# Two batches of triangular inverses moved from VectorE to GpSimd, and their closing transposes to a later place

## The chip, the cores and the metric

The kernel runs on one core of a Trainium2 chip. The metric is the device time of one execution in microseconds; less is better. Engines are named as in the profile: PE is TensorE, DVE is VectorE, ACT is ScalarE, POOL is GpSimd, SP is SyncE.

## What is computed

The kernel runs two blocks of a transformer one after the other, all in fp32, with 512 tokens and a width of 1024. The change lies in the mixer of an even layer of the second block. That mixer has two halves that read the same projections: a gated delta rule that runs over the tokens forward and backward, over a context of 256 tokens and the 512 latent tokens, and MLA, a softmax attention of 8 heads. The delta rule is computed in chunks of 64 tokens, and each chunk needs the inverse of a unit triangular matrix:

```python
m = jnp.where(strict, jnp.einsum('bhncd,bhnsd->bhncs', kb, kc) * decay, 0.0)
eye = jnp.eye(cl, dtype=f32)
tmat = lax.linalg.triangular_solve(m + eye, jnp.broadcast_to(eye, m.shape), left_side=True,
                                   lower=True, unit_diagonal=True)
u = jnp.einsum('bhncs,bhnsv->bhncv', tmat, vb)
w = jnp.einsum('bhncs,bhnsk->bhnck', tmat, kb * jnp.exp(gc)[..., None])
...
def step(s, inp):
    u_i, w_i, qk_i, qd_i, kd_i, gl_i = inp
    v_new = u_i - jnp.einsum('bhck,bhkv->bhcv', w_i, s)
    o_i = jnp.einsum('bhck,bhkv->bhcv', qd_i, s) + jnp.einsum('bhcs,bhsv->bhcv', qk_i, v_new)
    s = s * gl_i[..., None, None] + jnp.einsum('bhck,bhcv->bhkv', kd_i, v_new)
    return s, o_i
```

## The kernel before

The even layer's mixer starts with `even_in` (L1136), which runs the projections and convolutions and ends with the projections of L416. Beside its last units run the jobs of `gdn_chunks` (L1430). `decays(b)` (L1448) builds the matrices of one block of 128 tokens, and ScalarE copies their 32 x 32 diagonal parts into a batch tile (`triW`, L1489). There are three batches: "ctx", 0 (four latent blocks forward) and 1 (four backward). `inversion` transposes a batch on VectorE into the tile A (`triangles`, L1500) and inverts it: `invert` clears X and writes ones on its diagonal (L1505, L1506) and then, for j from 0 to 30, with n = j + 1 and m = 31 - j, multiplies a column of A with a row of X into the one buffer `tm` (L1510) and subtracts that from X (L1511), n times m elements on each of 128 partitions. A transpose (L1513) writes the result back into the batch's tile:

```python
t = gp.tile([128, 256], F32, name="tm", bufs=1)[:, :n * m].rearrange("p (y x) -> p y x", y=m)
V.tensor_tensor(t, X[:, j:j + 1, :n].to_broadcast([128, m, n]), A[:, n:, j:j + 1].to_broadcast([128, m, n]), OP.mult)
V.tensor_tensor(X[:, n:, :n], X[:, n:, :n], t, OP.subtract)
```

Batches 0 and 1 are the last job (L1522). Their tiles A and X are borrowed from the tiles eo0, eo1, eo2 (and a part of `triW`) that later hold the mixer's outputs.

`gdn_scan` (L1524) walks over the blocks, forward and backward side by side, in six walks; the walks 0 and 1 take the two context blocks, the walks 2 to 5 the latent blocks, so batches 0 and 1 are needed from walk 2 on. It has four tiles DT, two for each direction, which are cleared once (L1527). `solve(i)` copies the diagonal parts of the inverses into DT (L1546 on ScalarE, eight copies for a pair of blocks), completes them with two rounds of small products (`Dn`, L1556, `ng`, L1559 and L1563), and multiplies (`sa`, L1575). `step` (L1600) is one chunk of one direction, and its last instruction updates the state St (L1633).

Beside the walks runs `mla` (L1380), a generator that is advanced by one or two units after a walk. It goes over four pairs of heads p, and GpSimd issues its DMAs: the values `vp` (L1384, two buffers), the keys and queries `kq` of the two heads (L1388, 576 KB each, two buffers in all), and the stores of the results `boD` (L1419). TensorE computes the scores S (L1402) from kq. The context part of each result is cast into eo1 and eo3 (`hl`, L398 and L399).

The order of each engine's instructions is set by a scheduler that takes the program's instructions by readiness and priority; on the chip each engine then runs its queue in that order, each instruction waiting for what it needs. `tc.issue_after(x)` has the scheduler place what follows behind x.

Of the kernel before, what the change touches and what calls it, by code (L numbers as in the profile page):

```python
# [12 lines left out]
OP = mybir.AluOpType  # L13
# [225 lines left out]
def build(tc, A, out, cst_at, vec_at, chk_at, tap=None, upto=99, mark=lambda n: None):  # L239
    nc = tc.nc  # L240
    V, S, T, G = nc.vector, nc.scalar, nc.tensor, nc.gpsimd
# [53 lines left out]
    def bank(tag, cols, name):  # L295
        p, rings = state["pm"]
        return p.tile([128, cols], F32, name=name, tag=tag, bufs=rings[tag], padded_shape=[128, max(cols, 512)])
# [315 lines left out]
    x = xp.tile([128, KD, SEQ], F32, name="x", tag="x")  # L613
# [805 lines left out]
                    G.dma_start(boD[p, :, qb0:qb0 + 256], bt)  # L1419
                yield  # L1420

    batches, batch, inverse, NOc = {}, {}, {}, []

    def off_diagonal(d, a):

# [4 lines left out]
    def gdn_chunks(gp, slots):  # L1430
# [70 lines left out]

        def invert(key, A, X, Y):

            parts = batches[key][1]
            V.memset(X, 0.0)  # L1505
            V.memset(X.rearrange("p y x -> p (y x)")[:, ::33], 1.0)  # L1506
            for j in range(31):
                n, m = j + 1, 31 - j
                t = gp.tile([128, 256], F32, name="tm", bufs=1)[:, :n * m].rearrange("p (y x) -> p y x", y=m)
                V.tensor_tensor(t, X[:, j:j + 1, :n].to_broadcast([128, m, n]), A[:, n:, j:j + 1].to_broadcast([128, m, n]), OP.mult)  # L1510
                V.tensor_tensor(X[:, n:, :n], X[:, n:, :n], t, OP.subtract)  # L1511
            for d, r in parts:
                V.transpose(Y[r], X[r] if d == 0 else X[r].rearrange("p s c -> p c s"))  # L1513
            inverse[key] = Y

        def inversion(key, A, X):
            triangles(key, A)
            invert(key, A, X, batches[key][0])
# [4 lines left out]

    def gdn_scan(oT, gA, gp, beside, then):  # L1524
        DTs = [[gp.tile([128, 8, 128], F32, name=f"DT{d}{i}") for i in range(2)] for d in range(2)]
        for t in DTs[0] + DTs[1]:
            G.memset(t, 0.0)  # L1527
        prep = {}

        def solve(i):  # L1530
# [69 lines left out]
        def step(d, b, a, St):  # L1600

            u, wT, kd, eb, qd, qk = prep[d, b]
            rows = halves[a]

            pb = bank("step", 1024, "st").rearrange("p (b c) -> p b c", b=2)
            pw, po, pu = pb[:, :, :256], pb[:, a, 256:], pb[:, 1 - a, 256:]
            for p in range(4):
                for r in halves:  # L1610
                    T.matmul(po[r, 64 * p:64 * p + 64], St[r, p], qd[r, p, rows], start=p == 0, stop=False)
            for p in range(4):
                for half, r in enumerate(halves):
                    T.matmul(pw[rows, half, 64 * p:64 * p + 64], wT[r, p, rows], St[r, p], start=half != a, stop=half != a,
                             skip_group_check=half == a)
            vn = gp.tile([128, 8, 64], F32, name="vn", bufs=3)
            by = [v.rearrange("p (i b) t -> p i b t", b=2) for v in (vn[rows], u[rows])]
            V.tensor_tensor(by[0], by[1], pw[rows].rearrange("p b (i t) -> p i b t", i=4), OP.subtract)
            for h in range(8):
                T.matmul(pu[halves[h % 2], 64 * (h // 2):64 * (h // 2) + 64], kd[rows, h], vn[rows, h], start=True, stop=True)  # L1620
            for h in range(8):
                T.matmul(po[halves[h % 2], 64 * (h // 2):64 * (h // 2) + 64], vn[rows, h], qk[rows, 64 * h:64 * h + 64],
                         start=False, stop=h > 5)
            ot = oT[:, :, 128 * b + 64 * a:128 * b + 64 * a + 64]
            o3 = po.rearrange("p (i t) -> p i t", i=4)
            if (b, a) in seen:
                V.tensor_tensor(ot, o3, ot, OP.add)
            else:
                S.copy(ot, o3)
                seen.add((b, a))  # L1630
            last = 64 * a + (63 if d == 0 else 0)
            V.tensor_tensor(St, St, eb[:, :, last:last + 1].to_broadcast([128, 4, 64]), OP.mult)
            V.tensor_tensor(St, pu.rearrange("p (i t) -> p i t", i=4), St, OP.add)  # L1633

        St = []
        for d in range(2):
# [3 lines left out]
        order = [[4, 5, 0, 1, 2, 3], [5, 4, 3, 2, 1, 0]]  # L1640

        def walk(i):
            solve(i)
            for a in range(2):
                for d in range(2):
                    step(d, order[d][i], a if d == 0 else 1 - a, St[d])

        next(beside)
        for i in range(6):
            walk(i)  # L1650
            if i == 3:
                then()
            for _ in range(UNITS[i]):
                next(beside, None)
# [163 lines left out]
    def gated(sl, to, tile, ring, p):  # L1818
# [5 lines left out]
        for i, rb in zip(pairs, rsqrt_bcs(sqs, 2, 64, ring, p)):  # L1824
# [5 lines left out]

    gp = pool("gdn_b", gst, side="right")
    gdn_scan(oT, gA, gp, mla(pool("mla", mst, side="right"), [v[1] for v in os_[SEQ]]),
             lambda: gated(CT, [v[0] for v in os_[SEQ]], lambda n: gp.tile([128, 512], F32, name=n, tag=n, bufs=2), "turn", gp))
    mst.close()
# [52 lines left out]
    def begin(st):  # L1887
# [17 lines left out]
    order = [((4, 5, 6, 7, 8, 9), [CT]), ((0, 1, 2, 3), [PA]), ((1, 2, 3, 0), [PB]), ((10, 11, 16, 17), [LAT, CT]),  # L1905
             ((4, 5, 6, 7, 8, 9, 12, 13, 14, 15), [LAT])]
# [269 lines left out]
```

## Time and profile before

| | |
|---|---|
| median of 3 runs | 3221.37 us (3218.88 to 3226.10) |
| the profiled execution, its own time | 3223.53 us |
| its span | 3221.7 us |
| busy: TensorE, VectorE, ScalarE, GpSimd | 3067.8, 2041.2, 1448.2, 17.4 us |
| share of TensorE, of GpSimd in the chain that ended last | 62%, 0% |

The span is the time from the first to the last recorded instruction, and the profiled execution took 1.8 us more than its span. A row of a timeline gives start, duration, engine, line and operation, the tile written and the tiles read, and in brackets how long the engine stood idle before and what ended that. A row of a table by stretches gives, for one stretch of time, what the columns of its heading say. Each product of two fp32 operands has two records on TensorE.

### The profile page before, as it was taken

The numbers are of one execution on the slowest core, as the hardware profiler recorded it, in microseconds if no ns is written. First come the engines' busy times: TensorE is split into PE (matmuls) and PEld (weight loads), VectorE is DVE, ScalarE is ACT, GpSimd is POOL, SyncE is SP. The second block draws the span as 40 slices with busy tenths as digits, with TensorE's granted clock in tenths as the row PEclk, the third lists the DMA queues.
The fourth block names the chain that finished last, engine by engine and source line by source line (L and its number), as shares of the span: only waits on it lengthen the run. The fifth ranks groups of instructions, "written<-read, shape, count | busy, mean of one in ns | idle before, by whom it ended". The sixth has DMA issues, their size and how long they took to land.

```text
span 3221.7 us, 51374 instructions
## 1 busy us (share of the span) xinstructions
PE 3067.8 (95%) x20678; PEld 2605.9 (81%) x20678; DVE 2041.2 (63%) x4021; ACT 1448.2 (45%) x2533; POOL 17.4 (1%) x47
## 2 busy tenths in 40 slices
PE   6999999998999999998899999999997989999998
PEld 5788888975888889876667898888887867898887
DVE  7976555788787777668966674442338347572335
ACT  4965333446553335556554562212124446562223
POOL 0000000000000000000100000000000000000000
PEclk9999999997999999998999999999998999999999
DMA  7556554320266554442322433441223221242232
GB/s 233 190 155 218 194 189 163 125 66 7 74 195 200 188 198 166 131 143 96 107 67 92 142 105 118 165 136 58 67 69 125 79 91 47 76 152 95 95 100 101
DMA packets 137615, 404.11 MB, mean 125 GB/s; under 512 B 13856, under 2 KB 37152, under 8 KB 136736
## 3 DMA queue, kind: packets, MB, share of 16 engines
q1 hardware_dynamic: 135344, 389.81, 36.6%
q0 software_dynamic: 2032, 11.01, 1.1%
q8 instruction: 162, 2.65, 0.3%
q14 instruction: 77, 0.63, 0.1%
HBM read 376.12 MB, written 24.64 MB: 124 GB/s over the span
## 4 chain that ended last, share of the span: by engine, by line
PE 62%; issue 8%; DVE 5%; ACT 4%; DMA 0%; POOL 0%; DVEq 0%; ACTq 0%; POOLq 0%
PE mm L416 49%; PE po L1359 2%; PE rb L547 2%; PE ptr L1348 1%; PE S L830 1%; PE S L1402 1%; PE ss L527 1%; ACT DT L1546 1%; ACT wH L398 1%; PE po L969 1%; PE sa L1575 1%; PE ptr L975 1%; DVE acc L519 1%; DVE wL L399 1%; DVE ct L1683 0%
## 5 line engine op out<-in xcount | busy, mean ns | idle before, releaser
L398 ACT CAST wH<-raw 128x1024 fp32r<-128x1024 f32 (+4 forms) x446 | 451.8, 1015 | 1144.7 <-PE mm L416 786.0
L399 DVE TENSOR_TENSOR wL<-raw,wH 128x1024 fp32r<-128x1024 f32 (+4 forms) x446 | 525.1, 1180 | 377.4 <-ACT wH L398 370.5
L416 PE MATMUL mm<-mH,wH 128*128 128x256 f32 (+1 forms) x1280 | 406.8, 340 | 8.2 <-DVE f L1764 5.8
L416 PE MATMUL mm<-mH,wL 128*128 128x256 f32 (+1 forms) x1280 | 404.1, 339 | 1.9 <-DVE wL L399 1.9
L416 PE MATMUL mm<-mL,wH 128*128 128x256 f32 (+1 forms) x1280 | 404.2, 338 | 0.0
L416 PEld LDWEIGHTS mm<-mH,wH 128*128 128x128 f32 x1280 | 230.7, 190 | 39.5 <-ACT wH L398 6.0
L589 DVE SCALAR_TENSOR_TENSOR raw<-raw,cond_c 128x1024 f32<-128x1024 f32 x128 | 156.6, 1225 | 157.1 <-DMA raw<-in_ada 156.4
L416 PEld LDWEIGHTS mm<-mH,wL 128*128 128x128 f32 x1280 | 229.7, 189 | 30.9 <-DVE wL L399 2.3
L416 PEld LDWEIGHTS mm<-mL,wH 128*128 128x128 f32 x1280 | 230.2, 189 | 28.6
L416 PE MATMUL mm<-f2u0L,wH 128*128 128x512 f32 (+1 forms) x752 | 190.3, 327 | 0.0
L416 PE MATMUL mm<-f2u0H,wH 128*128 128x512 f32 (+1 forms) x752 | 190.0, 326 | 0.0
L416 PE MATMUL mm<-f2u0H,wL 128*128 128x512 f32 (+1 forms) x752 | 189.6, 326 | 0.0
L416 PE MATMUL mm<-f2u1H,wL 128*128 128x512 f32 (+1 forms) x432 | 151.4, 352 | 1.2 <-DVE wL L399 1.1
L416 PE MATMUL mm<-f2u1H,wH 128*128 128x512 f32 (+1 forms) x432 | 150.9, 352 | 0.6 <-ACT nt L1739 0.5
L416 PE MATMUL mm<-f2u1L,wH 128*128 128x512 f32 (+1 forms) x432 | 151.2, 352 | 0.2
L416 PEld LDWEIGHTS mm<-f2u0H,wL 128*128 128x128 f32 x752 | 118.1, 189 | 13.1
L416 PEld LDWEIGHTS mm<-f2u0H,wH 128*128 128x128 f32 x752 | 117.6, 189 | 12.9
L416 PEld LDWEIGHTS mm<-f2u0L,wH 128*128 128x128 f32 x752 | 117.7, 189 | 12.6
L1744 DVE TENSOR_TENSOR nt<-nt,mm 128x512 f32<-128x512 f32 (+1 forms) x52 | 31.5, 605 | 146.8 <-PE mm L416 146.4
L626 DVE SCALAR_TENSOR_TENSOR x<-mm,mod,x 128x256 f32<-128x256 f32 (+1 forms) x112 | 66.1, 597 | 88.5 <-PE mm L416 88.3
L416 PE MATMUL mm<-f0L,wH 128*128 128x512 f32 (+1 forms) x296 | 107.0, 362 | 0.5 <-DVE f0L L565 0.5
L416 PE MATMUL mm<-f0H,wH 128*128 128x512 f32 (+1 forms) x296 | 106.8, 361 | 0.4 <-ACT f0H L564 0.4
(697 smaller groups left out, 7232.9 us busy)
## 6 DMA issues: line engine op xcount, KB each, us to landing
raw<-in_ada SPq DMA_DIRECT2D x192, 512.0 KB, 3.8
raw<-in_fw SPq DMA_DIRECT2D x142, 512.0 KB, 4.1
raw<-in_gw SPq DMA_DIRECT2D x113, 512.0 KB, 3.3
raw<-in_gw SPq DMA_DIRECT2D x34, 384.0 KB, 3.0
raw<-in_owin SPq DMA_DIRECT2D x25, 512.0 KB, 3.2
raw<-in_ewin SPq DMA_DIRECT2D x22, 512.0 KB, 3.3
raw<-in_awin SPq DMA_DIRECT2D x20, 512.0 KB, 3.9
raw<-in_ewout SPq DMA_DIRECT2D x18, 512.0 KB, 3.4
```

Source lines behind the costliest of these rows:

```text
L398: S.copy(H, src)
L399: V.tensor_tensor(L, src, H.bitcast(F32), OP.subtract)
L416: T.matmul(ps, W[w][:, k], h(p, k0 + k, sl), start=first and k == 0 and j == 0, stop=last and k == kt - 1 and j == 2)
L519: V.tensor_tensor(acc[0], acc[0], sq, OP.add)
L527: T.matmul(pc[:, ns * b:ns * b + ns], sq, sel, start=True, stop=True)
L547: T.matmul(pb[r * i:r * i + r, b:b + 128], rs[:, c:c + 1].to_broadcast([128, r]), ident, start=True, stop=True)
L589: V.scalar_tensor_tensor(junk, r, 1.0, c, OP.mult, OP.mult, accum_out=o[:, j:j + 1])
L626: V.scalar_tensor_tensor(x[:, n, sl], ps, gate[:, n:n + 1], x[:, n, sl], OP.mult, OP.add)
L830: T.matmul(ps, q, k[:, sl], start=j == 0, stop=j == 1)
L969: T.matmul(po[64 * half:64 * half + 64], vw[:, kt, :64], PT, start=kt == 0, stop=kt == b)
L975: T.transpose(pt[:, 128 * i:128 * i + 128], Ps[half][i][:, 128 * kt:128 * kt + 128], ident)
L1359: T.matmul(po[64 * half:64 * half + 64], vs[half], PT[:kn, half * w:half * w + w], start=j == 0, stop=j == len(keys) - 1)
```

## The change

`invert` runs on GpSimd (G) for batches 0 and 1, and on VectorE (V) for the context's as before: 2 x 2 clears and 2 x 62 operations change engine. The closing transposes of the two batches are kept back in a list and issued, both together, before walk 2, behind the last state update of walk 1 (`step` returns its last instruction for that). Of the four tiles DT, the two that the first walk uses are cleared by VectorE, and the other two by GpSimd.

```diff
-    batches, batch, inverse, NOc = {}, {}, {}, []
+    batches, batch, inverse, NOc, late = {}, {}, {}, [], []
...
         def invert(key, A, X, Y):
 
-            parts = batches[key][1]
-            V.memset(X, 0.0)
-            V.memset(X.rearrange("p y x -> p (y x)")[:, ::33], 1.0)
+
+            E = V if key == "ctx" else G
+            E.memset(X, 0.0)
+            E.memset(X.rearrange("p y x -> p (y x)")[:, ::33], 1.0)
             for j in range(31):
                 n, m = j + 1, 31 - j
                 t = gp.tile([128, 256], F32, name="tm", bufs=1)[:, :n * m].rearrange("p (y x) -> p y x", y=m)
-                V.tensor_tensor(t, X[:, j:j + 1, :n].to_broadcast([128, m, n]), A[:, n:, j:j + 1].to_broadcast([128, m, n]), OP.mult)
-                V.tensor_tensor(X[:, n:, :n], X[:, n:, :n], t, OP.subtract)
-            for d, r in parts:
-                V.transpose(Y[r], X[r] if d == 0 else X[r].rearrange("p s c -> p c s"))
-            inverse[key] = Y
+                E.tensor_tensor(t, X[:, j:j + 1, :n].to_broadcast([128, m, n]), A[:, n:, j:j + 1].to_broadcast([128, m, n]), OP.mult)
+                E.tensor_tensor(X[:, n:, :n], X[:, n:, :n], t, OP.subtract)
+
+            def place():
+                for d, r in batches[key][1]:
+                    V.transpose(Y[r], X[r] if d == 0 else X[r].rearrange("p s c -> p c s"))
+                inverse[key] = Y
+            if key == "ctx":
+                place()
+            else:
+                late.append(place)
...
-        for t in DTs[0] + DTs[1]:
-            G.memset(t, 0.0)
+        for i in range(2):
+            for d in range(2):
+                (G if i else V).memset(DTs[d][i], 0.0)
...
+            return nc.cur_bb.bb.instructions[-1]
...
         def walk(i):
+            nonlocal done
+            if i == 2:
+                with tc.issue_after(done):
+                    for place in late:
+                        place()
             solve(i)
             for a in range(2):
                 for d in range(2):
-                    step(d, order[d][i], a if d == 0 else 1 - a, St[d])
-
+                    done = step(d, order[d][i], a if d == 0 else 1 - a, St[d])
+
+        done = None
         next(beside)
```

How this moves instructions shows at three places. First GpSimd's queue at the start of the scan, before the change, where the DT clears follow the last clear of `even_in` and MLA's DMAs follow them:

```order
L1204 MEMSET xb_11500 128x2 x3
L1527 MEMSET DT_14032 128x1024
L1527 MEMSET DT_14033 128x1024
L1527 MEMSET DT_14034 128x1024
L1527 MEMSET DT_14035 128x1024
L1384 DMA vp<-vD_t 128x768
L1388 DMA kq<-kqD_t 96x1536 x2
L1384 DMA vp<-vD_t 128x768
L1388 DMA kq<-kqD_t 96x1536
L1419 DMA boD_t<-bt 128x256
```

In the changed kernel (whose lines are numbered a little differently: L1511 and L1512 are the multiplication and the subtraction) the same queue holds batch 0's operations there, eo_12713 being its A and eo_12714 its X. Ahead of these rows stand 32 of them and the two DT clears:

```order
L1511 TENSOR_TENSOR tm<-eo_12714,eo_12713 128x255
L1384 DMA vp<-vD_t 128x768
L1512 TENSOR_TENSOR eo_12714<-eo_12714,tm 128x15x17
L1388 DMA kq<-kqD_t 96x1536
L1511 TENSOR_TENSOR tm<-eo_12714,eo_12713 128x252
L1388 DMA kq<-kqD_t 96x1536
L1512 TENSOR_TENSOR eo_12714<-eo_12714,tm 128x14x18
L1384 DMA vp<-vD_t 128x768
```

So the first loads of MLA stand among the operations of batch 0, behind 33 and 34 of them. What comes between these rows and the next DMA is the rest of batch 0 and the whole of batch 1 (X in eo_12712); the same queue at the end of batch 1:

```order
L1511 TENSOR_TENSOR tm<-eo_12712,triW 128x31
L1512 TENSOR_TENSOR eo_12712<-eo_12712,tm 128x31
L1388 DMA kq<-kqD_t 96x1536
L1419 DMA boD_t<-bt 128x256
L1388 DMA kq<-kqD_t 96x1536
L1384 DMA vp<-vD_t 128x768
```

The loads of the second pair of heads and the first store of a result stand behind all 124 operations. The third place is VectorE's queue at the end of walk 1 in the changed kernel:

```order
L1635 TENSOR_TENSOR oT<-st,oT 128x4x64
L1641 TENSOR_TENSOR St_14040<-st,St_14040 128x256
L1351 COPY PT<-ptr 128x512
L1516 STREAM_TRANSPOSE triW<-eo_12714 128x1024
L1516 STREAM_TRANSPOSE triW<-eo_12712 128x1024
L1415 TENSOR_TENSOR bt<-bt,rb 128x256
L1564 STREAM_TRANSPOSE Dn<-DT_14030 32x256 x2
L1564 STREAM_TRANSPOSE Dn<-DT_14032 32x256
```

Both closing transposes now stand behind the last state update of walk 1, and the transposes Dn of the next `solve` shortly behind them.

## Rows read from the trace of the kernel before

**Rows 1.** The page: busy us, share of the span and instructions of each engine

```profile
PE 3067.8 (95%) x20678; PEld 2605.9 (81%) x20678; DVE 2041.2 (63%) x4021; ACT 1448.2 (45%) x2533; POOL 17.4 (1%) x47
```

**Rows 2.** Table by stretches; its heading line names the columns

```profile
core 0: us, PE busy (x) PEld busy (x) DVE busy (x) ACT busy (x) POOL busy (x), PEclk, DMA share, GB/s
1530.00:1550.00 20.00, 9.83 (x162) 8.13 (x160) 17.73 (x51) 13.49 (x26) 5.66 (x8) 0.66 0.61 196
1550.00:1600.00 50.00, 48.35 (x631) 33.92 (x631) 46.21 (x159) 26.26 (x61) 1.59 (x3) 1.00 0.25 70
1600.00:1650.00 50.00, 43.55 (x580) 30.40 (x579) 39.41 (x120) 27.37 (x56) 2.69 (x5) 0.97 0.23 71
```

**Rows 3.** Table by stretches of L1510 alone (VectorE's busy us and count first after length)

```profile
1530.00:1622.45 92.45, 20.62 (x62) 0.93 0.33 101
```

**Rows 4.** The same of L1511

```profile
1530.00:1622.45 92.45, 20.82 (x62) 0.93 0.33 101
```

**Rows 5.** TensorE's waits, 1592 to 1645: us in total, times, longest

```profile
PE st L1620 <- DVE vn L1618: 1.0, 1, 1.0
PE S L1402 <- DVE P L1328: 0.3, 1, 0.3
PE st L1611 <- DVE tm L1510: 0.3, 1, 0.3
```

**Rows 6.** GpSimd's timeline, 1530 to 1600

```profile
1531.99 3.61 POOL L1527 MEMSET DT<- 128x1024 f32 x4 [234.53 <-PE mm L416]
1535.54 0.54 POOL L1384 DMA_DIRECT2D vp<-vD_t  x1
1536.07 1.02 POOL L1388 DMA_DIRECT2D kq<-kqD_t  x2
...
1584.87 0.52 POOL L1388 DMA_DIRECT2D kq<-kqD_t  x1 [47.22 <-PE S L1402]
```

**Rows 7.** GpSimd's groups by form (busy us, mean ns), and one line's semaphores (min/median/max ns)

```profile
L1527 POOL MEMSET DT<- 128x1024 f32 x4 | 3.6, 951 | 234.5 <-PE mm L416 234.5
...
L750 POOL MEMSET xb<- 128x3 f32 x10 | 0.9, 101 | 135.9 <-ACT wH L398 72.3 <-DVE xc L755 62.8 <-ACT cH L398 0.6
...
L750 POOLq EVENT_SEMAPHORE  x8: 42/43/43, 73.1 to 137.1; - x8
```

**Rows 8.** DMA issues, 1530 to 1610: count, size, median us from issue to landing

```profile
kq<-kqD_t POOLq DMA_DIRECT2D x4, 576.0 KB, 5.3
```

**Rows 9.** TensorE's timeline around the first scores of each pair of heads

```profile
1547.12 1.68 PE L1402 MATMUL S<-kq 96*128 96x256 f32 x4
...
1588.48 0.75 PE L1563 MATMUL ng<-DT,ND 32*32 32x32 f32 x64 [0.47 <-ACT ND L1560]
...
1590.87 0.94 PE L1575 MATMUL sa<-VK,DT 128*128 128x128 f32 x6
...
1592.19 0.39 PE L1575 MATMUL sa<-VK,DT 128*128 128x128 f32 x2
1592.42 1.03 PE L1402 MATMUL S<-kq 96*128 96x256 f32 x4
```

**Rows 10.** VectorE's timeline: closing transposes of the context, opening one of batch 0

```profile
1507.80 3.22 DVE L1513 STREAM_TRANSPOSE triW<-eo 64x1024 f32<-64x1024 f32 x2
...
1526.29 1.23 DVE L1500 STREAM_TRANSPOSE eo<-triW 128x1024 f32<-128x1024 f32 x1
```

**Rows 11.** ScalarE's timeline: the copies into DT for walk 2

```profile
1624.50 5.13 ACT L1546 COPY DT<-triW 32x256 f32<-32x256 f32 x8 [1.53 <-DVE triW L1513]
```

**Rows 12.** TensorE's timeline after an idle stretch in even_in

```profile
1490.04 0.77 PE L416 MATMUL mm<-eH,wH 128*128 128x512 f32 x1 [5.55 <-DVE NTs L1481]
...
1492.10 0.63 PE L416 MATMUL mm<-eL,wH 128*128 128x512 f32 x1
...
1493.93 0.40 PE L416 MATMUL mm<-eL,wH 128*128 128x512 f32 x1
```

**Rows 13.** VectorE's groups by form, 1530 to 1605: busy us, mean ns

```profile
L1569 DVE TENSOR_TENSOR kd<-k,kdw 128x512 f32<-128x512 f32 x5 | 3.4, 681 | 0.0
L1567 DVE TENSOR_TENSOR VK<-k,egc 128x512 f32<-128x512 f32 x5 | 3.4, 676 | 0.0
```

## The prediction

> **What bounds the kernel now.** I read the page first: TensorE is busy for 95% of the span, VectorE for 63%, GpSimd for 1% [rows 1]. That is an average over many stages, so I next read the table by stretches of the stage that the change touches, the first two walks of the scan. In the 50 us from 1550 to 1600, while VectorE works off the two batches, TensorE is busy for 48.35 us and VectorE for 46.2 us [rows 2]: both are nearly full, and TensorE is what the time follows. The same view of the two lines of the inversions shows what would leave VectorE: 62 multiplications and 62 subtractions in the stretch of the two batches, 20.6 + 20.8 = 41.4 us, or 0.334 us each [rows 3, 4]. What that is worth is in the list of TensorE's waits behind it: from 1592 to 1645, VectorE ended waits of 1.0, 0.3 and 0.3 us [rows 5], 1.6 us altogether. So 41 us of VectorE's work hold TensorE up for less than 2.
>
> The other side is the queue that receives the work. In the timeline of GpSimd the reader sees that it is no idle queue in this stage: it issues the loads vp and kq, from which MLA's scores are computed, at 1535.5 and 1536.1, and the first kq of the next pair of heads at 1584.9 [rows 6]. A kq load takes 5.3 us from issue to landing [rows 8]. TensorE's timeline has the first scores at 1547.1 and the first of the second pair at 1592.4 [rows 9].
>
> **Price of one operation on GpSimd.** The trace has no elementwise operation with two inputs on GpSimd, so I bound it. A batch is 62 operations on 10,912 elements of a partition (n times m, summed over j, twice), 176 on average. GpSimd's memsets cost 0.101 us for 3 elements and 0.951 for 1024 [rows 7], that is 0.10 fixed and 0.83 ns an element. Low end: one stream like the memset's, 0.10 + 176 x 0.83 ns = 0.25 us. Taken value: two reads and a write one after another, 2.49 ns an element, and 0.14 fixed, since each operation waits on GpSimd's own semaphore for the one ahead and a semaphore instruction there took 0.04 [rows 7]; that is 0.44 + 0.14 = 0.58 us, 35.9 us a batch. High end: a fixed part like that of the DMA issue, 0.52 us [rows 6], 0.44 + 0.52 = 0.96 us. VectorE's 0.334 lies inside. I take 0.58 because the memset row is the only arithmetic-like work of this engine and a program that has to fetch two inputs and write one cannot be nearer to it than three streams unless they overlap; how far they overlap is what I don't know. By the Trainium skill (GPSIMD Engine Reference, section 3.1 Elementwise) a tensor_tensor takes GpSimd 1.96 times as long as VectorE (4497 against 2293 ns for 2048 elements); an estimate by that page is 0.334 x 1.96 = 0.65 us, and the sum would come to about 3248; no run so far shows it.
>
> **The change, part by part.**
>
> 1. *124 operations leave VectorE.* Gain: the three waits, -1.6 us [rows 5]. Low end nothing; for more than that see the first rival.
>
> 2. *124 operations enter GpSimd's queue ahead of MLA's loads.* They start when the input of batch 0 is transposed, 1526.3 + 1.2 = 1527.5 [rows 10]. The order puts 33 of them ahead of the first vp and 34 ahead of the first kq. Those 33 have 5967 elements: 5967 x 2.49 ns + 33 x 0.14 = 19.5 us; the 34th, with 255, takes 0.8. Two DT clears (0.9 each [rows 6]) and the issue of vp (0.5) stand there too: kq is issued at 1527.5 + 19.5 + 1.8 + 0.5 + 0.8 = 1550.1 and lands at 1555.4. TensorE has the score matmuls at the same place of its queue as before, after four products of solve, and comes there at 1547.1 [rows 9]: it stands still for 8.3 us, and everything behind in its queue with it. VectorE and ScalarE run out of work soon after, so nothing is caught up.
>
>  The rest of batch 0 and all of batch 1 then run before the first kq of the second pair is issued. The last operation ends at 1527.5 + 2 x 35.9 + 1.8 + 2.1 (four DMA issues) = 1603.2; kq lands at 1608.5. TensorE's order has its first score matmul ahead of the second product of solve(1) and eight sa products that stood ahead of it before; these took 0.75 + 0.94 + 0.39, about 2.0 us between starts [rows 9], so TensorE comes there 2.0 earlier than at 1592.4: at 1590.4, plus the 8.3 already lost. It stands for 1608.5 - 1598.7 = 9.8 us. The two stalls together are 18.1 us, and this sum depends only on the second landing: 124 x price + 9.2 us of clears, issues and landing after 1527.5, against 1590.4. At 0.25 us nothing is left of it; at 0.96 it is 65 us.
>
> 3. *TensorE's clock after a stall.* After an idle of 5.55 us at 1490 a 512-column product took 0.77 and then 0.63 us, and 0.40 again from 1493.9 on [rows 12]: the granted clock had fallen to the lower of its two levels, 1.2 GHz, and 3.9 us at 0.63 instead of 0.40 cost 1.4 us. The first stall falls in a stretch with a low granted clock before as well (0.66 [rows 2]), so I count one: +1.4 us, between 0 and 2.8.
>
> 4. *The closing transposes wait for the end of walk(1) and stand in a row.* Two of them in a row, of half height, took 3.2 us [rows 10]; behind them come eight copies of ScalarE, 5.1 us [rows 11], before walk(2) can be solved. Before, the last transpose ended at 1624.5 [rows 11] and the copies ran beside the last steps of walk(1). Now 8.3 us of chain begin when walk(1) ends. What covers them is MLA's work of two units, which the stalls have left over: TensorE has the second pair's scores and products still to do. I count 0, between -2 and +4. If the cover is gone (inversions ready early, MLA ahead), the 4 us is what remains of it.
>
> 5. *The DT clears.* Two of 0.95 us go to VectorE while it waits for even_in's end, 0. ScalarE's ninth copy now waits for GpSimd's two; it falls in the first stall, 0. If that cover is gone, the first 21 operations and the clears put them some 13 us after 1527.5, still ahead of the first stall's end.
>
> 6. *The first result of MLA's context part (a cast into eo1 on ScalarE) overwrites batch 0's input,* and so waits for batch 0's last operation, 1527.5 + 35.9 + 3.9 = 1567.3; before, it came in the middle of walk(0), and the first stall moves it back by 8.3 us: 0. At 0.96 it is 0 too, since the first stall grows with batch 0. An extra instruction in GpSimd's queue ahead of the first operation runs between the context transposes' end at 1511.0 and 1527.5 [rows 10], 16 us of cover: 0.
>
> Sum on the profiled execution: 3223.5 + 18.1 + 1.4 - 1.6 = 3241.4. It was 2.2 above the median of the three runs, 3221.4, so the forecast is 3239 for the median.
>
> **The rivals.** In the neighbourhood of the forecast a hundredth of a microsecond in the price is worth 1.2 us, so the rivals are prices with a mechanism.
>
> *Faster: GpSimd streams.* If the two reads and the write overlap and the price is below 0.34, the first kq lands before 1547 and the second before 1579: no stall. VectorE loses 41 us of work, and in the most favourable case all of TensorE's idle time between 1550 and 1650 goes with it, (50 - 48.35) + (50 - 43.55) = 8.1 us [rows 2]. That gives 3213; the point from which it decides is the price of 0.34. For it speaks that GpSimd's memset does an element in 0.83 ns; against it, that VectorE itself, which has to read two inputs as well, needs 0.334 for the same operations.
>
> *No change: GpSimd is about as fast as VectorE,* 0.34 to 0.48. At 0.43 the second kq lands in time and the first is 3 us late, which the 1.6 us of gained waits half pay back: about 3222. At 0.48 the sum is 3227.
>
> *Slower still: VectorE shuts GpSimd out.* Nothing in the trace shows the two at work at once. If VectorE's operations with two inputs in SBUF hold GpSimd up for their own length, the two largest groups alone, VK and kd, add 6.8 us by 1605 [rows 13], and the sum is 3246; prices of 0.62 to 0.71 give 3244 to 3255. The Trainium skill says so (SBUF — State Buffer, section SBUF: two separate sides): GpSimd and VectorE share a port pair under an exclusive lock, taken by a VectorE operation with two SBUF inputs against a GpSimd operation that reads SBUF. By that rule the inversions and most of the scan's VectorE work exclude each other; the trace before can't show it.
>
> *Much slower: the fixed part is large.* Small operations pay a fixed cost each time. Half way between 0.10 and 0.52 the price is 0.75 and the sum 3260; at the end of the bound, 3286.
>
> **How the numbers follow.** Faster case 0.09, no change 0.18, forecast (0.48 to 0.62, that is 3227 to 3244) 0.43, shut out 0.20, large fixed part 0.10. The range leaves out the first and the last, 0.19: from 3217, the -1.6 of part 1 and the -2 of part 4 below the unchanged 3221.4, to 3256, a price of 0.71. A measurement of this kernel tells 0.2%, 6.4 us, from no change: faster 0.09, same 0.18, slower 0.73.
>
> **What would show it.** GpSimd's timeline: the mean of the new operations, 0.58, and the end of the last at about 1603. TensorE's waits: one of 8 us for kq at the first score matmul and one of 10 at the second pair's, with later work of the stage shifted by 18 to 20 us. VectorE's busy time in 1530 to 1625 down by about 41. The forecast is wrong if the mean is below 0.43, if TensorE waits in walk(1) or walk(2) for something other than kq (the transposes, the copies into DT), or if MLA's loads stand elsewhere in time than the order says.

## The result and the profile after

The changed kernel takes 3252.15 us (median of four runs, 3250.16 to 3258.46) against 3223.49 us for the kernel before in the same session. The ratio is 1.0095 with a 95% interval of 1.0083 to 1.0108: slower by about 29 us. That is inside the range given, 3217 to 3256, and on the side that was forecast, but 13 us above the forecast of 3239. The profiled execution took 3250.72 us, with a span of 3248.9.

The page of the changed kernel, engines and chain [rows 1]:

```profile
PE 3074.7 (95%) x20678; PEld 2610.8 (80%) x20678; DVE 2013.8 (62%) x3895; ACT 1449.1 (45%) x2533; POOL 87.1 (3%) x173
...
PE 67%; DVE 6%; ACT 4%; POOL 2%; issue 2%; DMA 0%; DVEq 0%; ACTq 0%; POOLq 0%
```

GpSimd has 70 us more of work, VectorE 27 less, and GpSimd, which had no share of the chain that ended last, has 2%. That VectorE has 27 us less and not the 41 of the prediction is a matter of counting: records of instructions that follow each other on VectorE overlap (before the change a row that starts at 1530.90 and lasts 0.68 us is followed by one at 1531.50), and busy time counts each moment once. Without the records of the 124 operations VectorE's busy time before would be 2014.9 us instead of 2041.2, so they filled 26.3. The same stretches as before, in the table by stretches [rows 2]:

```profile
core 0: us, PE busy (x) PEld busy (x) DVE busy (x) ACT busy (x) POOL busy (x), PEclk, DMA share, GB/s
1530.00:1550.00 20.00, 5.77 (x141) 4.48 (x139) 9.90 (x18) 12.74 (x23) 18.27 (x28) 0.61 0.20 69
1550.00:1600.00 50.00, 42.12 (x465) 30.36 (x465) 27.75 (x81) 18.74 (x42) 44.44 (x78) 0.88 0.27 83
1600.00:1650.00 50.00, 36.70 (x451) 26.50 (x447) 20.70 (x67) 16.82 (x39) 10.03 (x23) 0.83 0.22 64
```

VectorE's busy time between 1550 and 1600 has gone from 46.21 to 27.75 us, as it should. TensorE's has gone from 48.35 to 42.12, and its mean granted clock from 1.00 to 0.88: the engine that bounds the stage stands more and runs slower. What it waits for, in the list of its waits from the end of even_in to 1660 (total, times, longest):

```profile
PE S L1402 <- DMA kq<-kqD_t: 19.9, 2, 13.1
PE ng L1567 <- DVE Dn L1564: 6.4, 4, 3.6
PE ng L1571 <- ACT ND L1568: 6.0, 1, 6.0
```

Two waits for kq, 19.9 us together, which did not exist before. GpSimd's timeline has the reason [rows 6]:

```profile
1526.30 0.25 POOL L1511 TENSOR_TENSOR tm<-eo,eo 128x31 f32<-128x31 f32 x1 [15.62 <-DVE eo L1500]
...
1539.12 0.95 POOL L1535 MEMSET DT<- 128x1024 f32 x1
...
1549.85 0.60 POOL L1384 DMA_DIRECT2D vp<-vD_t  x1
...
1551.09 0.53 POOL L1388 DMA_DIRECT2D kq<-kqD_t  x1
...
1608.39 0.25 POOL L1512 TENSOR_TENSOR eo<-eo,tm 128x31 f32<-128x31 f32 x1
1608.94 0.55 POOL L1388 DMA_DIRECT2D kq<-kqD_t  x1 [0.30 <-issue]
```

The first kq is issued at 1551.1 instead of 1536.1, the first of the second pair at 1608.9, right behind the last of the 124 operations, instead of 1584.9. TensorE's score matmuls start when these land [rows 9]:

```profile
1556.60 2.07 PE L1402 MATMUL S<-kq 96*128 96x256 f32 x4 [6.79 <-DMA kq<-kqD_t]
...
1614.07 2.04 PE L1402 MATMUL S<-kq 96*128 96x256 f32 x4 [13.13 <-DMA kq<-kqD_t]
```

One more figure is used below, the **stage**: from the end of even_in's last product (L416) on TensorE to the start of ScalarE's last copy of an MLA result (L1414). It leaves out the code before and behind, which took between 2951 and 2967 us in the profiled executions of the runs below; a stage and a median can therefore differ by several microseconds on the same edit. Before it is 1532.0 to 1798.3, 266.3 us; after, 1530.7 to 1824.7, 294.0 us. The 27.7 us between them are the whole difference of the two profiled executions (27.2).

### The profile page after: what moved, and what is told of

It is laid out like the page before. It is cut to its first block, busy times and chain, and to the rows that moved or that the text cites. A ratio compares the mean times of both kernels' runs of the same rounds, so it can differ in the third digit from the quotient of the medians.

```text
span 3248.9 us, 51390 instructions
## 1 busy us (share of the span) xinstructions
PE 3074.7 (95%) x20678; PEld 2610.8 (80%) x20678; DVE 2013.8 (62%) x3895; ACT 1449.1 (45%) x2533; POOL 87.1 (3%) x173
## 4 chain that ended last, share of the span: by engine, by line
PE 67%; DVE 6%; ACT 4%; POOL 2%; issue 2%; DMA 0%; DVEq 0%; ACTq 0%; POOLq 0%
PE mm L416 53%; PE rb L547 2%; PE po L1359 2%; PE ptr L1348 1%; PE S L830 1%; PE ss L527 1%; POOL eo L1512 1%; POOL tm L1511 1%; PE S L1402 1%; PE po L969 1%; ACT wH L398 1%; PE ptr L975 1%; PE sa L1583 1%; DVE wL L399 1%; DVE c L1227 1%
## 5 line engine op out<-in xcount | busy, mean ns | idle before, releaser
L416 PE MATMUL mm<-mH,wH 128*128 128x256 f32 (+1 forms) x1280 | 407.1, 340 | 8.6 <-DVE f L1779 5.8
L416 PE MATMUL mm<-mH,wL 128*128 128x256 f32 (+1 forms) x1280 | 404.5, 339 | 1.5 <-DVE wL L399 1.5
L416 PE MATMUL mm<-mL,wH 128*128 128x256 f32 (+1 forms) x1280 | 404.5, 338 | 0.0
L416 PEld LDWEIGHTS mm<-mH,wH 128*128 128x128 f32 x1280 | 230.9, 190 | 39.7 <-ACT wH L398 6.1
L416 PEld LDWEIGHTS mm<-mH,wL 128*128 128x128 f32 x1280 | 230.0, 190 | 30.7 <-DVE wL L399 2.1
L416 PEld LDWEIGHTS mm<-mL,wH 128*128 128x128 f32 x1280 | 230.6, 190 | 28.5
L416 PE MATMUL mm<-f2u0L,wH 128*128 128x512 f32 (+1 forms) x752 | 190.3, 327 | 0.0
L416 PE MATMUL mm<-f2u0H,wH 128*128 128x512 f32 (+1 forms) x752 | 190.0, 326 | 0.0
L416 PE MATMUL mm<-f2u0H,wL 128*128 128x512 f32 (+1 forms) x752 | 189.6, 326 | 0.0
L416 PE MATMUL mm<-f2u1H,wL 128*128 128x512 f32 (+1 forms) x432 | 151.5, 352 | 1.2 <-DVE wL L399 1.1
L416 PE MATMUL mm<-f2u1H,wH 128*128 128x512 f32 (+1 forms) x432 | 151.0, 352 | 0.6 <-ACT nt L1754 0.5
L416 PE MATMUL mm<-f2u1L,wH 128*128 128x512 f32 (+1 forms) x432 | 151.2, 352 | 0.1
L416 PEld LDWEIGHTS mm<-f2u0H,wL 128*128 128x128 f32 x752 | 118.0, 189 | 13.2
L416 PEld LDWEIGHTS mm<-f2u0H,wH 128*128 128x128 f32 x752 | 117.8, 189 | 12.9
L416 PEld LDWEIGHTS mm<-f2u0L,wH 128*128 128x128 f32 x752 | 117.7, 189 | 12.6
L416 PE MATMUL mm<-f0H,wH 128*128 128x512 f32 (+1 forms) x296 | 106.8, 361 | 0.4 <-ACT f0H L564 0.4
L416 PE MATMUL mm<-f0L,wH 128*128 128x512 f32 (+1 forms) x296 | 106.9, 361 | 0.2 <-DVE f0L L565 0.2
```

The source lines that it names most:

```text
L416: T.matmul(ps, W[w][:, k], h(p, k0 + k, sl), start=first and k == 0 and j == 0, stop=last and k == kt - 1 and j == 2)
```

## The experiments

The theory that went into the first four runs, A, is the prediction's: the loss is where MLA's loads stand in GpSimd's queue. Its rival, B, is that the inversions themselves come too late or disturb VectorE.

**The loads taken out of the queue.** Changed kernel with this edit:

```diff
-            G.dma_start(vp, vD[p])
+            load(vp, vD[p])
...
-                G.dma_start(kq, kqD[2 * p + half])
+                load(kq, kqD[2 * p + half])
```

> The changed kernel with MLA's loads vp and kq issued by SyncE instead of GpSimd; the inversions stay on GpSimd. Theory A (the time is lost where MLA's loads stand behind GpSimd's operations): TensorE's two waits for kq, 6.8 and 13.1 us, are gone, the last GpSimd operation still ends near 1608, and the time is 3218 to 3226, some 27 below the changed kernel; the wait of 6.0 us for ND, which comes from the DT clears in GpSimd's queue, now costs about 2.7 in the open. Theory B (the inversions themselves come too late or slow VectorE down, through the transposes, the copies behind them or a shared port): the loads don't matter and the time stays at 3245 to 3255.

Measured: 3240.93 us, ratio to the kernel before 1.0050 (1.0038 to 1.0062). 11 us of the 29 are gone, not 27. The waits for kq are gone, as theory A has it, but others are there, in the lists of waits of ScalarE, VectorE and TensorE up to 1660. The one for ND was in the changed kernel too, the two at the cast into eo were 1.2 and 0.9 us there, and the last is new:

```profile
ACT eo L398 <- POOL tm L1511: 5.7, 1, 5.7
...
DVE eo L399 <- ACT eo L398: 5.6, 1, 5.6
...
PE ng L1571 <- ACT ND L1568: 6.0, 1, 6.0
PE sa L1583 <- ACT eb L1599: 4.3, 1, 4.3
```

and walk 2 is long: the last of its four state updates ends at 1703.2, 58.8 us after walk 1's, against 45.0 before. Neither theory had that alone.

**The control:** the kernel before with the same edit.

> The control to the first run: the kernel before with the same loads on SyncE. Both theories: the loads were in time already, so 3220 to 3226, no difference beyond 0.1%. If it is faster or slower by more, the first run has to be read against this one and not against the kernel before.

Measured: 3225.11 us, 1.0004 (0.9993 to 1.0015). SyncE's queue is as good a place for these loads, and no better.

**Everything but GpSimd:** the changed kernel with `E = V` for all batches; the late transposes and the moved clears stay.

> The changed kernel with both batches back on VectorE: only the late transposes and the moved DT clears are left of the change. Theory A: 3220 to 3227, since the chain of 3.1 us of transposes and eight copies at the start of walk 2 is mostly covered by MLA's work. Theory B in the form that the late transposes cost the time: 3230 to 3250.

Measured: 3230.55 us, 1.0018 (1.0008 to 1.0028), 6.8 us slower than the kernel before and above what A allowed. Its profiled stage is 265.7 us, no longer than before, while the code before and behind took 9.7 us longer in that execution, so the profile doesn't show where the 6.8 lie; that is left open. What they belong to is asked again in e12_clears_alone.

**One batch on GpSimd:**

```diff
-            E = V if key == "ctx" else G
+            E = G if key == 1 else V
...
-            if key == "ctx":
+            if key != 1:
                 place()
```

> The changed kernel with batch 0 back on VectorE and only batch 1 on GpSimd. The first loads of MLA then stand ahead of all GpSimd operations, and the first kq of the second pair behind some 36 of the 62. Theory A: it lands before 1575, TensorE waits for no kq, and the time is 3217 to 3225. Theory B: half the operations, half the loss, about 3237.

Measured: 3246.78 us, 1.0073 (1.0060 to 1.0086). A miss of 22 us, and the reason is plain in GpSimd's timeline:

```profile
1579.87 0.25 POOL L1511 TENSOR_TENSOR tm<-eo,triW 128x31 f32<-128x31 f32 x1 [41.89 <-DVE eo L1512]
...
1602.36 0.56 POOL L1388 DMA_DIRECT2D kq<-kqD_t  x1
```

I had batch 1 start at 1530. Both batches write the one buffer `tm`, so GpSimd waits until VectorE has done with batch 0, at 1579.7, and the second pair's kq, behind 36 of its operations, is issued at 1602.4. TensorE waits 11.7 us for it. With half of the operations the kernel loses nearly as much, 23.0 us of 28.7; 11.7 us of TensorE's wait for kq, against 19.9, are part of that, and the two moved clears and batch 1's late transpose are in this run too. What sets the wait is when the queue comes to the load, not how much work is in it.

**Theory C** was formed from these: three parts, the loads behind GpSimd's operations, the DT clears behind them (ScalarE's ninth copy and with it ND wait for these), and the closing transposes at the end of walk 1. Its rival D: what e1 had left is MLA's units and the walks out of step. The first edit moves all clears to VectorE, `V.memset(DTs[d][i], 0.0)`; the second places the transposes early:

```diff
-            if i == 2:
+            if i == 1:
                 with tc.issue_after(done):
-                    for place in late:
-                        place()
+                    late[0]()
...
                     done = step(d, order[d][i], a if d == 0 else 1 - a, St[d])
+                    if i == 1 and a == 0 and d == 0:
+                        with tc.issue_after(done):
+                            late[1]()
```

> The loads on SyncE as in e1_loads_sync, and all four DT clears on VectorE instead of two behind GpSimd's operations. Theory C (the loss has three parts: the loads behind GpSimd's operations, the DT clears behind them at the start, and the closing transposes at the end of walk 1): ScalarE's ninth copy no longer waits 2.7 us for a clear, TensorE's wait of 6.0 us for ND shrinks to about 2, and the time is 3235 to 3239, some 4 below e1_loads_sync. Theory D (what is left in e1_loads_sync is lost in walk 2 because MLA's units and the walks have come out of step): 3240 to 3243.

Measured: 3235.97 us, 1.0041 (1.0028 to 1.0054): 5 us below e1, the time that C has. The place is another than C's, though. TensorE's wait for ND shrinks to 4.0 us and the first sa product comes 1.9 us earlier after even_in's end than in e1, but ScalarE then waits 9.8 us instead of 5.7 for GpSimd at the cast into eo1, and walk 1 ends 110.2 us after even_in's end in both runs. The stage is shorter in walk 2, 49.5 us against 58.8; why is not shown.

> The loads on SyncE as in e1_loads_sync, and the closing transposes placed as soon as the batches are there: batch 0's behind the last update of walk 0, batch 1's behind the first of walk 1. Theory C: the copies into DT for walk 2 run beside walk 1 again, walk 2 shrinks from 59 us to 45 to 48, and the time is 3226 to 3233. Theory D: 3238 to 3243.

Measured: 3230.87 us, 1.0019 (1.0010 to 1.0029): 10 us below e1, as C has it. Walk 2 is down to 41.8 us. One row each of the table by stretches, from the end of walk 1's last state update to that of walk 2, of e1 and then of e8 (columns as above):

```profile
1644.40:1703.20 58.80, 53.42 (x750) 40.57 (x745) 29.65 (x72) 34.39 (x71) 1.08 (x2) 0.80 0.20 59
```

```profile
1642.10:1683.90 41.80, 38.78 (x585) 28.05 (x585) 23.82 (x65) 22.19 (x49) 1.08 (x2) 1.00 0.33 96
```

With the late transposes TensorE's mean granted clock in walk 2 is 0.80, with the early ones 1.00. Not all of the 17 us are won: TensorE has 750 instructions in the first stretch and 585 in the second, since MLA's units fall into other walks, and the stage is 11.5 us shorter. The copies into DT explain the start of it: in the changed kernel both transposes and eleven of the copies run in a row once walk 1 is over, on VectorE and then ScalarE:

```profile
1660.02 3.09 DVE L1516 STREAM_TRANSPOSE triW<-eo 128x1024 f32<-128x1024 f32 x2
```

```profile
1661.35 7.07 ACT L1554 COPY DT<-triW 32x256 f32<-32x256 f32 x11
```

> The changed kernel with the transposes placed early, as in e8_sync_early, and MLA's loads left on GpSimd. Theory C: both waits for kq stay (about 20 us), walk 2 shrinks by up to 8 us, and the time is 3241 to 3248. Theory D: 3250 to 3255.

Measured: 3244.82 us, 1.0071 (1.0055 to 1.0086): 7 us below the changed kernel, with 21.0 us of waits for kq still there. D has failed three times.

> The three edits together: loads on SyncE, all clears on VectorE, transposes early; the inversions stay on GpSimd. Theory C: the parts add up, 3220 to 3228, the level of the kernel before; below 3218 would mean that VectorE's 41 us are worth something after all. Theory D: 3235 to 3241.

Measured: 3231.87 us, 1.0030 (1.0018 to 1.0042). A miss: the parts do not add up, the clears bring nothing once the transposes are early. ScalarE's, VectorE's and TensorE's lists of waits up to 1660 show what took their place:

```profile
ACT eo L398 <- POOL tm L1511: 9.3, 1, 9.3
...
DVE eo L399 <- ACT eo L398: 9.2, 1, 9.2
...
PE S L1402 <- DVE P L1328: 8.7, 1, 8.7
```

The first context result of MLA goes into eo1, which still holds the input of batch 0; ScalarE reaches that cast 9.3 us before GpSimd has read it for the last time. In e1 and e8 it was 5.7 us, since a late start brought ScalarE there later, in e7 9.8, and in the changed kernel 1.2, since TensorE had been waiting for kq.

**A start as before.** All clears on GpSimd at the head, and both inversions issued behind them (the loads on SyncE and the transposes early as in e8):

```diff
+                todo.append(lambda: invert(key, A, X, batches[key][0]))
...
-        for i in range(2):
-            for d in range(2):
-                (G if i else V).memset(DTs[d][i], 0.0)
+        for t in DTs[0] + DTs[1]:
+            G.memset(t, 0.0)
+        with tc.issue_after(nc.cur_bb.bb.instructions[-1]):
+            for job in todo:
+                job()
```

> As e8_sync_early (loads on SyncE, transposes early), but with all four DT clears on GpSimd as in the kernel before, and both inversions issued behind them, so that the start of the scan is as before. Theory C: the first sa product comes 13 us after even_in's last product as before (17 with the change), walk 1 and walk 2 take what they took in e8_sync_early, and the time is 3219 to 3225: the three parts are then all undone, and with 124 operations still on GpSimd the kernel is no slower than before. If it stays at 3229 or above, what is left belongs to the inversions on GpSimd themselves (a shared port, or walk 1 waiting for them). A gain of more than 0.2%, below 3217, would mean that taking 41 us off VectorE is worth something, which the waits before (1.6 us) deny.

Measured: 3237.52 us, 1.0045 (1.0030 to 1.0059). The start is as before, the first sa product 13.2 us after even_in's last, but the inversions now end later, ScalarE's cast waits 10.5 us for them and TensorE stands once for 9.4. So this run moved the loss and did not separate the start. At 3229 or above the rest was to belong to the inversions on GpSimd themselves; the two waits say in what form: they end too late for the cast.

**The clears alone,** in the kernel before.

> The kernel before with one edit: two of the four DT clears on VectorE, in the changed order. Theory C: VectorE comes to its clears late and ScalarE runs all 16 copies ahead of ND, so the start is 4 us longer, of which MLA's and the walks' slack gives some back: 3224 to 3229. If it is at 3224 or below, the 6.8 us of e4_all_but_gpsimd were the late transposes'.

Measured: 3228.52 us, 1.0023 (1.0014 to 1.0032), as C has it: 6 us slower from two clears that change engine, in a kernel where nothing else does. TensorE's two waits at the start are now for Dn, 6.6 us, and ND, 4.0, against 5.6 and 1.5 before. VectorE's first clear stands behind ten operations of batch 0, starts at 1536.8, and ScalarE's copies wait 3.0 us for it. By the expectation's rule the 6.8 us of e4_all_but_gpsimd are then not the late transposes': the clears alone cost 6.2, and with the inversions on VectorE no cost of the late transposes is to be seen. (The stages do not repeat this: 272.9 us here, 265.7 there.)

**The cast moved away.** In `mla` the context unit of each pair of heads goes behind the two latent units, on top of e9, and for a control on the kernel before:

```diff
-            for qb0, nk, k0, b0 in ((SEQ, CTX, SEQ, 4), (0, TOT, 0, 0), (256, TOT, 0, 0)):
+            for qb0, nk, k0, b0 in ((0, TOT, 0, 0), (256, TOT, 0, 0), (SEQ, CTX, SEQ, 4)):
```

> As e9_sync_clears_early, with the context unit of MLA moved behind the two latent units of each pair of heads, so that the first cast into eo1 comes some 35 us later and batch 0's input is no longer in use by then. Theory E (the rest of the loss is that ScalarE stands 9.3 us at this cast for GpSimd's last operation on batch 0, VectorE 9.2 us behind it, and TensorE 8.7 us): these waits vanish and the time falls by about 8 us against e9_sync_clears_early, to 3222 to 3226, level with the kernel before. Theory F (the rest is the shared port, or the start): 3229 to 3233.

> The control to the run above: the kernel before with the context unit last and nothing else. Both theories: the same work in another order, 3219 to 3228; what it differs by from the kernel before is to be taken off the run above.

Measured: the control 3219.89 us, 1.0003 (0.9994 to 1.0012), no difference. On e9's kernel 3235.78 us, 1.0045 (1.0031 to 1.0058), where 3222 to 3226 was expected. The waits for the cast are gone, and another wait of the same kind stands there, in the same three lists:

```profile
ACT bt L1414 <- DMA boD_t<-bt: 12.7, 1, 12.7
...
DVE bt L1415 <- ACT bt L1414: 13.1, 1, 13.1
...
PE ng L1571 <- ACT ND L1568: 14.9, 2, 10.9
```

`bt` has two buffers. Their stores, boD, are issued by GpSimd and stand behind the inversions until 1608.4; ScalarE waits for a buffer, ND stands behind it on ScalarE, and TensorE behind ND. Theory E was right on the cast and wrong on what remains: the next item of GpSimd's queue. No run has the stores on SyncE too.

All runs in one table; each stage is worked out from two rows of its trace (where the context unit is last, the stage ends with another piece of work and is not given).

| | us | against before | stage |
|---|---|---|---|
| before | 3223.5 | | 266.3 |
| changed | 3252.2 | +28.7 | 294.0 |
| e10: transposes early | 3244.8 | +20.9 | 289.1 |
| e5: one batch on GpSimd | 3246.8 | +23.0 | 287.2 |
| e1: loads on SyncE | 3240.9 | +17.2 | 283.0 |
| e7: and clears on VectorE | 3236.0 | +12.0 | 275.0 |
| e8: loads on SyncE, transposes early | 3230.9 | +6.9 | 271.5 |
| e9: all three | 3231.9 | +7.9 | 271.7 |
| e11: e8, start as before | 3237.5 | +15.2 | 277.3 |
| e13: e9, context last | 3235.8 | +15.6 | |
| e4: nothing on GpSimd | 3230.6 | +6.8 | 265.7 |
| e12: before, two clears moved | 3228.5 | +6.2 | 272.9 |
| e2: before, loads on SyncE | 3225.1 | +1.4 | 263.7 |
| e14: before, context last | 3219.9 | -0.3 | |

(Against the median of the kernel before in the same session.) No version with inversions on GpSimd is faster than the kernel before.

## Why the prediction was right, and where it was short

**The bound, and part 1: right as far as the runs show.** No run has a gain from taking the inversions off VectorE. In e8 and e9, where GpSimd's queue holds neither loads nor late transposes up, walk 1 takes 48.2 and 48.1 us against 48.0 before; walk 0 is about 10 us longer there, for reasons given below, so that a gain as small as the 1.6 us of part 1 could not be seen. The list of waits that part 1 was read from begins at 1592. From 1532 to 1592 VectorE ended further waits of TensorE, 7.0 us for Dn; the changed kernel still has 6.4 of them, so they did not come from the inversions.

**Part 2, the mechanism: right, with its size short by 6 us.** The places were those forecast: a wait at the first scores and one at the second pair's, 6.8 and 13.1 us, and the last operation at 1608.6 (1603.2 forecast). The landing of the second pair's first kq set the end, 1614.1 instead of 1608.5. Against the 1590.4 at which TensorE would have come there that is 23.7 us instead of 18.1. The term that was mis-sized is the price of an operation: 0.58 was taken, and from 1526.30 to 1608.64, less the two clears and four issues (4.1 us), 124 operations took 0.631 us each.

**The price, and the third rival.** An operation on 31 elements took 0.24 to 0.25 us and one on 256 took 0.64 to 0.73 where nothing disturbed it: 0.18 fixed and 1.8 to 2.1 ns an element, with 0.08 between one and the next. Three streams of 0.83 ns had been taken as 2.49 ns, which is too much, and the fixed part was 0.26 where 0.14 was taken. Undisturbed that is 0.585 us, close to the forecast, and by luck: the two errors nearly cancel at 176 elements. The rest, 0.046, is the third rival. Twelve of the 124 operations took 0.32 to 0.67 us longer than the fastest of their line and size, 5.7 us over all 124; beside each stood an operation of VectorE with two inputs in SBUF, and in eight of the twelve that, too, took longer (0.72 to 1.17 us) than the 0.68 us of its form in [rows 13]. One such case, GpSimd's row, a row of the same form without VectorE beside it, and VectorE's row:

```profile
1575.66 0.86 POOL L1512 TENSOR_TENSOR eo<-eo,tm 128x175 f32<-128x175 f32 x1
```

```profile
1563.14 0.53 POOL L1512 TENSOR_TENSOR eo<-eo,tm 128x175 f32<-128x175 f32 x1
```

```profile
1575.10 1.03 DVE L1575 TENSOR_TENSOR VK<-k,egc 128x512 f32<-128x512 f32 x1
```

The two hold each other up, as the Trainium skill (SBUF — State Buffer, section SBUF: two separate sides) says; the trace agrees, and its size is near the 6.8 us of the rival. It touched twelve of the 124 operations, though, and not, as the prediction has it, most of the scan's VectorE work. The price as a whole, 0.631, lies in the rival's band, 0.62 to 0.71. The prediction's sentence that nothing in the trace before shows the two engines at work at once is wrong: GpSimd's four clears ran from 1531.99 to 1535.60 [rows 6] beside VectorE, and took no longer there than in the changed kernel (0.95 us); it is for operations with two inputs that it showed nothing. By the Trainium skill (GPSIMD Engine Reference, section 3.1 Elementwise) the ratio to VectorE is 1.96, measured on 2048 elements; at the sizes here the trace has 0.56 against 0.334 us in the mean length of a record, 1.67. GpSimd's 0.631, from which the prediction's sum goes, is counted from start to start.

**Part 4: wrong in size.** The late transposes were put at 0, between -2 and +4, with MLA's left-over work as cover. e10 against the changed kernel has 7 us and e8 against e1 has 10; in the changed kernel's stage it is 4.9. What was left out is that the copies for walk 3 come in the same rush as those for walk 2, and that TensorE's clock falls with the waits in between, 0.80 in the mean over walk 2 in e1. In the changed kernel itself TensorE waits 1.2 us for a Dn and 0.8 for a copy into DT at the start of walk 2, the sign that the prediction named for this, and its clock is at the lower level behind them:

```profile
1670.00:1675.00 5.00, 4.23 (x74) 2.80 (x74) 1.99 (x9) 4.85 (x13) 0.00 (x0) 0.50 0.08 21
```

**Parts 5 and 6: right only for the cover named.** Both waits were in the changed kernel as said: ScalarE waited 2.7 us for a DT clear and 1.2 us for batch 0's last operation, and both were hidden by the first wait for kq. Without that cover they cost: in e1 and e8 the first sa product comes 17.0 and 17.1 us after even_in's end instead of 13.2, and the cast is followed by a wait of 8.7 us on TensorE in e9. What part 5 says of the two clears on VectorE, 0, holds for the changed kernel to within a microsecond: they start at 1531.34 and 1532.42, and ScalarE waits 0.8 us for them. In e12 they cost 6 us, since the inversions stand ahead of them in VectorE's queue there, and 16 copies instead of 14 come ahead of ND on ScalarE.

**Part 3, the clock, was short as well.** TensorE's table by stretches after the second wait:

```profile
1610.00:1620.00 10.00, 5.93 (x50) 3.95 (x50) 1.76 (x8) 2.27 (x6) 0.57 (x2) 0.51 0.46 131
```

The granted clock was 0.51, the lower of its two levels, while 5.9 us of products ran; at full clock they would have taken about 3 us less by an estimate (half of them), where 1.4 was counted.

**What adds up.** Stage, against before: 22.8 us with the transposes early (e10), and 4.9 for the late transposes, 27.7. The second landing is the whole of the 22.8. In e10 the second pair's first score starts 84.1 us after even_in's end, instead of the 58.4 (1590.4) at which TensorE would have come there, 25.8 later with about 3 regained behind it:

```profile
1615.39 1.19 PE L1402 MATMUL S<-kq 96*128 96x256 f32 x2 [13.60 <-DMA kq<-kqD_t]
```

The remaining 5 us of stage in e8 and e9 lie in walk 0, while GpSimd inverts. Its row in the table by stretches, from the end of even_in to the last state update, before and then in e8 and e9:

```profile
1532.04:1587.40 55.36, 44.13 (x633) 31.92 (x634) 49.87 (x165) 31.40 (x65) 6.68 (x10) 0.88 0.33 97
```

```profile
1528.69:1593.90 65.21, 45.04 (x570) 33.49 (x571) 35.20 (x94) 30.82 (x65) 58.00 (x97) 0.82 0.29 89
```

```profile
1532.27:1597.30 65.03, 45.74 (x573) 33.27 (x573) 36.17 (x92) 29.70 (x62) 57.58 (x96) 0.82 0.27 80
```

It is 9.9 and 9.7 us longer, though TensorE has fewer instructions in it, and its clock is lower; walk 2 and what follows give back 4 to 5. Two losses are together of this size: the later start of the sa products (3.9 and 2.1 us) and TensorE's wait right behind the cast that waits for batch 0's last operation (4.3 and 8.7). What the experiments did not settle is how much of this would go if the cast came in time: e13 took its wait away, but brought the stores' wait. Nor is the shared port's part told apart; it reaches TensorE only by making batch 0 end later, and the lengthened operations of batch 0 add up to about 3 us in the changed kernel.

## What to carry to other kernels

An idle engine is not free if its queue carries others' transfers: before moving work to it, list what its queue issues during that time (loads, stores, clears) and work out when the queue comes to each. Here no run shows a gain from what was taken off VectorE, TensorE stood 19.9 us for the loads behind the new work, and moving these loads won back only 11, since each wait that was taken away uncovered the next one behind the same queue. A late consumer placed "where it costs nothing" should be priced with everything that then comes in a rush behind it, copies for later steps and the clock included.

## What was not expected of the hardware

GpSimd does an operation with two inputs on 31 to 256 elements at 0.18 us plus 1.8 to 2.1 ns an element, so that by the length of a record it takes only 1.3 to 1.7 times as long as VectorE (0.24 and 0.19 us for 31 elements, 0.64 to 0.73 and 0.42 for 256). And the mutual hold-up with VectorE is small: 5.7 us of the 69.4 us for which GpSimd was busy with these operations, with VectorE busy for 27.75 of the 50 us from 1550 to 1600 beside them.
